# Sort steps of a graph-attention kernel: a row step in three instructions, and a third key buffer

## The chip, the cores and the metric

The kernel runs on one core of one Trainium2 chip. The metric is the device time of one execution in microseconds (us). DVE is the vector engine, ACT the scalar engine, PE the matrix engine, POOL the GpSimd engine and SP the sync engine; each works through its own queue in program order.

## What is computed

A graph-attention layer over 4096 nodes of 64 features, 50,000 random edges and 4 heads. Cut to what matters:

```python
x_proj[h] = x @ weight[h]
score[h, i] = leaky_relu(att_src[h] . x_proj[h, src[i]] + att_dst[h] . x_proj[h, dst[i]], 0.2)
output[h, dst[i]] += exp(score[h, i]) * x_proj[h, src[i]]        # over all edges i
output[h, d] /= sum(exp(score[h, i]) for edges i with dst[i] == d) + 1e-8
```

The order in which edges are added up is free, so the kernel sorts them into groups of source and destination nodes first.

## The kernel before

The edges lie as 391 keys in each of 128 partitions (`EL` = 391, padded to `L` = 512 columns with a large constant). A bitonic network sorts them: `rows` sorts every partition by itself, `runs` merges the rows of 4 neighbouring partitions, the sorted keys go to memory (`store`), parts of them are fetched again by indirect DMAs (`fetch`, on POOL), and a second stage (`pairs`, `rows(9)`, `runs`) sorts those. After it 32 blocks of destination nodes are worked through: one-hot matrices on DVE, gathers and sums as matmuls on PE, copies on ACT.

A step of the network compares two halves of each block of 2h columns. `flip` (line 197) opens a merge level k and reads the second half backwards, `half` (line 206) does the steps below it. Each step is two DVE `tensor_tensor` instructions over the whole width, first the minimum, then the maximum, and goes from one of two buffers, `sA` and `sB`, to the other. The next step reads what both wrote. `rows(1, EL)` (line 236, called in line 786) runs the levels k = 1 to 9. Levels 1 to 3 (6 steps) are 392 columns wide, levels 4 to 7 (22 steps) 384, because 391 is less than 8 over a multiple of 128; level 8 opens with a `flip` over all 512 columns, which takes up the 8 columns left out (lines 199 to 204, width `L`). An instruction handles one half of each block, so its width in elements is 196 or 192 in levels 1 to 7 and 256 in the `flip` of level 8.

All instructions are issued in the order in which the program names them (`manual_schedule`). On POOL this order is: constants (lines 87 to 156), two small DMAs of padding (lines 160, 163), a memset of `below` (line 291), and then what `tables` (line 408, called in line 785, one line ahead of `so.rows`) puts there: a memset, eight DMAs into `attbd` (line 419), a memset, and four DMAs into `Wbd` (line 424). `rows` itself puts nothing on POOL; the next POOL instruction is the `fetch` after the first sort.

The waits between instructions, also between two on one engine, are generated from the regions of the tiles that they read and write.

Of the kernel before, what the change touches and what calls it, by code (L numbers as in the profile page):

```python
# [16 lines left out]
OP = mybir.AluOpType  # L17
# [17 lines left out]
def av(a, off, *dims):  # L35

    return dataclasses.replace(a, offset=a.offset + off, ap=[list(a.ap[0])] + [list(d) for d in dims])
# [3 lines left out]
def kernel(ctx: ExitStack, tc: tile.TileContext, x: bass.AP, edge_index: bass.AP,  # L41
                         weight: bass.AP, att_src: bass.AP, att_dst: bass.AP, out: bass.AP):
    nc = tc.nc
    V, S, G, T = nc.vector, nc.scalar, nc.gpsimd, nc.tensor
# [135 lines left out]
    class Sorter:  # L180


        def __init__(self, pool):
            self.a = [None, pool.tile([P, L], F32, name="sA"), pool.tile([P, L], F32, name="sB")]
            self.y = pool.tile([P, L], F32, name="sY")
            self.z = pool.tile([P, L], F32, name="sZ")

        def begin(self, first):
            self.a[0] = first
            self.cur = 0  # L190
# [36 lines left out]
        def opposed(self, j):  # L227
# [4 lines left out]
            for o, op in ((0, OP.min), (h, OP.max)):  # L232
                V.scalar_tensor_tensor(out=av(d[:], o, [2 * h, n], [1, h]), in0=av(s[:], h, [2 * h, n], [1, h]),
                                       scalar=-1.0, in1=av(s[:], 0, [2 * h, n], [1, h]), op0=OP.mult, op1=op)

        def rows(self, first, n=L):

            w8 = -(-n // 8) * 8
            w128 = n // 128 * 128 if n % 128 <= 8 else L
            for k in range(first, 10):  # L240
                w = w8 if k <= 3 else w128 if k <= 7 else L
                self.flip(k, w)
                for j in range(k - 2, -1, -1):
                    self.half(j, w if k <= 7 or j > 6 else w128 if j > 2 else w8)
                if k == 3:
                    kept = self.cur
                if k == 7 and first <= 3:
                    assert self.cur == kept

        def turn(self):  # L250

# [33 lines left out]
    def store(skey, t):  # L285
        nc.sync.dma_start(out=skey[0, 0:P * L].rearrange("(p e) -> p e", p=P), in_=t[:])

    def below(pool, v, n, nbnd, nt, room):

        sgn = pool.tile([P, room + 1], F32, name="sgn")  # L290
        G.memset(sgn[:, 0:1], float(n))
        junk = pool.tile([P, n], F32, name="junk")
        for b in range(1, nt + 1):
            S.activation(out=junk[:], in_=v, func=ACTF.Sign, bias=nbnd[:, b:b + 1], scale=1.0,  # L294
                         accum_out=sgn[:, b:b + 1])
        if room > nt:
            S.copy(out=sgn[:, nt + 1:room + 1], in_=av(sgn[:], nt, [0, room - nt]))
        return sgn

    def counts(pp, sgn, nt, sels):  # L300

        ps = pp.tile([P, len(sels), nt + 1], F32, name="cnt_ps")
        for i, sel in enumerate(sels):
            T.matmul(out=ps[:, i, :], lhsT=sel, rhs=sgn[:], start=(i == 0), stop=True, skip_group_check=True)  # L304
        return ps

    def bounds(pool, ps):

        cnt = pool.tile([P, SETS, NR + 1], F32, name="cnt")
        pick = [pool.tile([P, SETS, NR], F32, name=f"pick{o}") for o in range(2)]  # L310
        sum = [pool.tile([P, SETS], F32, name=f"sum{o}") for o in range(2)]
        sides = (ws1, we1)
        steps = [lambda: V.tensor_scalar(out=cnt[:], in0=ps[:], scalar1=-0.5, scalar2=RUN1 * EL / 2, op0=OP.mult,
                                         op1=OP.add)]
        for f in (lambda o: V.tensor_tensor(out=pick[o][:], in0=cnt[:, :, o:o + NR],
                                            in1=av(m16[:], 0, [0, SETS], [1, NR]), op=OP.mult),
                  lambda o: V.tensor_reduce(out=sum[o][:], in_=pick[o][:], axis=AX, op=OP.add),
                  lambda o: V.tensor_tensor(out=sides[o][:], in0=sum[o][:], in1=off1[:], op=OP.add)):
            steps += [lambda f=f, o=o: f(o) for o in range(2)]
        steps.append(lambda: V.tensor_copy(out=wi1[:], in_=ws1[:]))  # L320
        return [lambda keys, f=f: f() for f in steps]
# [436 lines left out]
    key = cst.tile([P, L], F32)  # L758
    raw = cst.tile([P, L], F32)
    so = Sorter(cst)  # L760
    first = ExitStack()
    so1 = first.enter_context(tc.tile_pool(name="sort1", bufs=1))
    pr = first.enter_context(tc.tile_pool(name="pre", bufs=1))
    with tc.tile_pool(name="pps", bufs=2, space=PSUM) as pps, tc.tile_pool(name="pp1", bufs=1, space=PSUM) as pp1:
        sli = so1.tile([P, EL], I32)
        uF = so1.tile([P, EL], F32)
        dF = so1.tile([P, EL], F32)
        kF = so1.tile([P, EL], F32)
        so.begin(key)
        for t in (key, so.a[2]):  # L770
            V.memset(t[:, EL:L], KPAD)
        sgn = below(so1, av(eS[:], 0, [2, EL]), EL, nb1, NR, NR)
        for e, n in ((0, EH), (EH, EL - EH)):
            src = av(eS[:], 2 * e, [2, n])
            dst = av(eD[:], 2 * e, [2, n])
            c = slice(e, e + n)

            V.tensor_scalar(out=sli[:, c], in0=src, scalar1=2 * N - SG, scalar2=None, op0=OP.bitwise_and)
            V.tensor_scalar(out=dF[:, c], in0=dst, scalar1=float(N // 2), scalar2=-float((N - 1) * SG), op0=OP.is_ge,
                            op1=OP.mult)  # L780
            V.scalar_tensor_tensor(out=uF[:, c], in0=sli[:, c], scalar=float(N - 1), in1=src, op0=OP.mult, op1=OP.add)
            V.scalar_tensor_tensor(out=kF[:, c], in0=dst, scalar=float(2 * SG), in1=dF[:, c], op0=OP.mult, op1=OP.add)
            V.tensor_tensor(out=key[:, c], in0=uF[:, c], in1=kF[:, c], op=OP.add)
        cps = counts(pp1, sgn, NR, [sel1[:, i, :] for i in range(SETS)])
        tables(pr, pps, pp1)
        so.rows(1, EL)
        store(skey1, so.runs(RUN1, between=bounds(so1, cps)))
# [129 lines left out]
```

## Time and profile before

| | |
|---|---|
| time, median of 3 runs | 277.17 us (276.71 to 280.39) |
| the profiled execution: time, span | 276.81 us, 275.0 us |
| busy: PE, DVE, ACT, POOL | 74%, 91%, 68%, 15% of the span |
| `tensor_tensor` of line 212 (both buffers) | 202 instructions, 70.2 us |

The busy shares are means over stages of different kind. The first 57 us are the sort, where DVE is busy nearly throughout; from about 122 us on PE and DVE are both busy nearly throughout with the blocks.

### The profile page before, as it was taken

The numbers are of one execution on the slowest core, as the hardware profiler recorded it, in microseconds if no ns is written. First come the engines' busy times: TensorE is split into PE (matmuls) and PEld (weight loads), VectorE is DVE, ScalarE is ACT, GpSimd is POOL, SyncE is SP. The second block draws the span as 40 slices with busy tenths as digits, with TensorE's granted clock in tenths as the row PEclk, the third lists the DMA queues.
The fourth block names the chain that finished last, engine by engine and source line by source line (L and its number), as shares of the span: only waits on it lengthen the run. The fifth ranks groups of instructions, "written<-read, shape, count | busy, mean of one in ns | idle before, by whom it ended". The sixth has DMA issues, their size and how long they took to land.

```text
span 275.0 us, 8348 instructions
## 1 busy us (share of the span) xinstructions
PE 204.5 (74%) x3455; PEld 191.8 (70%) x3455; DVE 250.3 (91%) x521; ACT 186.1 (68%) x381; POOL 42.1 (15%) x83
## 2 busy tenths in 40 slices
PE   0011699992000197779999999999999999999992
PEld 0011479992000044579999999999999999999991
DVE  5999999935999999779999999999999999999991
ACT  1980550007999805787887888888888888888861
POOL 7885000014000000602314033000000000000000
PEclk9999995555555589999999999999999999999998
DMA  4008000011000000187394954976687768566011
GB/s 116 0 2 170 4 0 2 0 38 39 0 0 0 0 2 31 47 325 318 107 396 154 378 203 149 375 269 238 212 299 249 279 216 303 213 263 244 23 42 44
DMA packets 12763, 39.53 MB, mean 144 GB/s; under 512 B 2160, under 2 KB 8496, under 8 KB 8880
## 3 DMA queue, kind: packets, MB, share of 16 engines
q1 hardware_dynamic: 10176, 36.78, 36.4%
q10 hardware_dynamic: 1840, 1.58, 2.4%
q0 software_dynamic: 704, 0.59, 1.0%
q8 instruction: 28, 0.46, 0.7%
q14 instruction: 15, 0.12, 0.1%
HBM read 33.96 MB, written 4.98 MB: 142 GB/s over the span
## 4 chain that ended last, share of the span: by engine, by line
PE 54%; DVE 34%; DMA 5%; ACT 2%; issue 2%; POOL 0%; DVEq 0%; SPq 0%; POOLq 0%
PE acc L630 20%; DVE sA L212 13%; DVE sB L212 12%; PE ps L543 10%; PE pf L710 6%; PE ps L541 6%; PE ps L547 6%; PE acc L620 4%; DMA bc<-gat_bins 2%; DMA eS<-in_edge_index_dram 1%; DVE sA L201 1%; DVE sB L253 1%; ACT bc L508 1%; DMA raw<-gat_sorted,wi 1%; DVE sA L203 1%
## 5 line engine op out<-in xcount | busy, mean ns | idle before, releaser
L551 ACT CAST xs<-ps 128x1200 bf16<-128x1200 f32 (+1 forms) x96 | 100.8, 1050 | 0.0
L567 DVE TENSOR_TENSOR val<-xs,wv 128x4096 bf16<-128x4096 bf16 x30 | 68.4, 2281 | 0.1
L630 PE MATMUL acc<-xs,val 128*128 128x128 bf16 x992 | 60.7, 219 | 0.1
L543 PE MATMUL ps<-adb,oh 128*128 128x136 bf16 x512 | 59.5, 223 | 0.0
L541 PE MATMUL ps<-xa,oh 128*128 128x72 bf16 x512 | 56.9, 196 | 2.2 <-ACT bc L508 1.1
L630 PEld LDWEIGHTS <-val 128*128 128x128 bf16 x992 | 56.0, 98 | 0.6 <-DVE val L567 0.5
L543 PEld LDWEIGHTS <-oh 128*128 128x128 bf16 x512 | 47.5, 98 | 1.5 <-issue 1.4
L541 PEld LDWEIGHTS <-oh 128*128 128x128 bf16 x512 | 45.5, 98 | 1.4 <-DVE oh L520 1.4
L520 DVE TENSOR_SCALAR oh<-bc,pF 128x4096 bf16<-128x4096 bf16 (+2 forms) x36 | 41.1, 1141 | 2.8 <-ACT bc L508 1.8
L304 PE MATMUL cnt_ps<-sgn,sel 128*128 128x17 f32 (+1 forms) x10 | 2.5, 379 | 51.5 <-issue 31.9
L304 PEld LDWEIGHTS cnt_ps<-sgn,sel 128*128 128x128 f32 x10 | 2.3, 325 | 51.5 <-issue 51.5
L549 ACT ACTIVATE ex<-ps 128x96 bf16<-128x96 f32 (+1 forms) x96 | 24.3, 253 | 20.0 <-PE ps L547 19.9
L212 DVE TENSOR_TENSOR sA<-sB 128x256 f32<-128x256 f32 (+3 forms) x102 | 35.4, 388 | 1.5
L212 DVE TENSOR_TENSOR sB<-sA 128x256 f32<-128x256 f32 (+3 forms) x100 | 34.8, 389 | 1.5
L547 PE MATMUL ps<-xa,oh 128*128 128x72 bf16 x512 | 32.3, 197 | 0.0
L547 PEld LDWEIGHTS <-oh 128*128 128x128 bf16 x512 | 25.5, 99 | 0.1
L446 PEld LDWEIGHTS at_ps<-uv,xT 64*128 64x128 f32 x128 | 25.2, 304 | 0.2 <-issue 0.2
L446 PE MATMUL at_ps<-uv,xT 64*128 64x4 f32 x128 | 25.3, 334 | 0.0
L522 DVE TENSOR_SCALAR oh<-bc,pF 128x2048 bf16<-128x2048 bf16 (+2 forms) x36 | 24.9, 691 | 0.0
L294 ACT ACTIVATE junk<-kr,nb 128x512 f32<-128x512 f32 x32 | 23.1, 722 | 1.1
L710 PE MATMUL pf<-Wbd,aT 128*128 128x128 f32 x124 | 21.2, 293 | 0.0
L620 PEld LDWEIGHTS <-xs 128*128 128x128 bf16 x496 | 17.4, 96 | 0.4
(148 smaller groups left out, 248.9 us busy)
## 6 DMA issues: line engine op xcount, KB each, us to landing
bc<-gat_bins SPq DMA_DIRECT2D x30, 1024.0 KB, 5.9
out_dram<-res SPq DMA_DIRECT2D x31, 128.0 KB, 3.5
eD<-in_edge_index_dram ACTq DMA_DIRECT2D x2, 195.0 KB, 4.0
eS<-in_edge_index_dram SPq DMA_DIRECT2D x2, 195.0 KB, 3.8
gat_sorted<-sA SPq DMA_DIRECT2D x1, 256.0 KB, 2.0
gat_sorted<-ki SPq DMA_DIRECT2D x1, 256.0 KB, 2.0
gat_bins<-tb SPq DMA_DIRECT2D x4, 64.0 KB, 1.9
attbd<-in_att_src_dram POOLq DMA_DIRECT2D x4, 0.2 KB, 4.7
```

The lines of the kernel that those rows point to most:

```text
L212: V.tensor_tensor(out=av(d[:], at + o, [2 * h, n], [1, h]), in0=av(s[:], at, [2 * h, n], [1, h]), in1=av(s[:], at + h, [2 * h, n], [1, h]) ...
L446: T.matmul(out=ps[:, b, :], lhsT=nodes(b), rhs=uv[:, k, :], start=(b == 0), stop=True, skip_group_check=True)
L520: V.tensor_scalar(out=oh[:, e], in0=bc[:, e], scalar1=pF[:, 0:1], scalar2=None, op0=OP.is_equal)
L522: V.tensor_scalar(out=av(oh[:], (2 * NT + t0) * W2, [W2, nt], [1, W2]), in0=av(bc[:], (2 * t0 + 1) * W2, [2 * W2, nt], [1, W2]), scalar1=p ...
L541: T.matmul(out=ps[:, i, P:P + XC], lhsT=hot(2 * t + 1), rhs=xa[:, 2 * t, :], start=(i % 2 == 0), stop=False, skip_group_check=True)
L543: T.matmul(out=ps[:, i, 0:S0], lhsT=hot(2 * t), rhs=adb[:, b, :], start=False, stop=False, skip_group_check=True)
L547: T.matmul(out=ps[:, i, P:P + XC], lhsT=hot(2 * NT + t), rhs=xa[:, 2 * t + 1, :], start=False, stop=True, skip_group_check=True)
L551: S.copy(out=xs[:, t0:t0 + n, 0:P + XC], in_=ps[:, 0:n, 0:P + XC])
L567: V.tensor_tensor(out=av(val[:], 0, [Dout, H], [C, NT], [1, Din]), in0=av(xs[:], S0, [0, H], [XW, NT], [1, Din]), in1=av(wv[:], 0, [2, H * ...
L620: T.matmul(out=self.acc[:, 2 * BD:AW], lhsT=xs[:, t, 0:P], rhs=av(wv[:], 2 * (t - t0), [2 * n, H]), start=(t == 0), stop=(t == NT - 1), sk ...
L630: T.matmul(out=self.to[k], lhsT=val[:, t, k * P:(k + 1) * P], rhs=xs[:, t, 0:BD], start=False, stop=(t == NT - 1), skip_group_check=True)
L710: T.matmul(out=self.pf[0:t.shape[-1], k * P:(k + 1) * P], lhsT=t, rhs=Wbd[:, k, :], start=(k == 0), stop=True, skip_group_check=True)
```

## The change

In `rows`, levels 1 to 7 no longer use `flip` and `half` but a new `apart`. It issues three instructions instead of two: the minimum over the left 192 columns (128 in level 7), the maximum over all columns, and the minimum over the columns that are left. The buffers become three (`sA`, `sB`, and `sZ`, which `runs` uses as scratch later), taken in turn. Levels 8 and 9 keep `flip` and `half` over `sA` and `sB`. After level 3 the keys lie in the third buffer and the 8 columns that levels 4 to 7 leave out are copied from it to `sA` by a POOL instruction (`G.tensor_copy`), since level 7 ends in `sA` and level 8 reads it there. The padding of the second buffer moves to `sA`.

```diff
+            self.a.append(self.z)
...
+        def apart(self, k, j, width):
+
+
+            s, self.cur = self.a[self.cur], self.cur % 3 + 1
+            d = self.a[self.cur]
+            h = 1 << j
+            n = width // (2 * h)
+            m = (128 if k == 7 else 192) // (2 * h)
+            mirror = j == k - 1
+            for b, c, op in ((0, m, OP.min), (0, n, OP.max), (m, n - m, OP.min)):
+                at = 2 * h * b
+                o = h if op == OP.max else 0
+                if mirror:
+                    in0 = av(s[:], at + o, [2 * h, c], [1, h])
+                    in1 = av(s[:], at + 2 * h - 1 - o, [2 * h, c], [-1, h])
+                else:
+                    in0 = av(s[:], at, [2 * h, c], [1, h])
+                    in1 = av(s[:], at + h, [2 * h, c], [1, h])
+                V.tensor_tensor(out=av(d[:], at + o, [2 * h, c], [1, h]), in0=in0, in1=in1, op=op)
...
             for k in range(first, 10):
                 w = w8 if k <= 3 else w128 if k <= 7 else L
-                self.flip(k, w)
-                for j in range(k - 2, -1, -1):
-                    self.half(j, w if k <= 7 or j > 6 else w128 if j > 2 else w8)
+                if k <= 7:
+                    for j in range(k - 1, -1, -1):
+                        self.apart(k, j, w)
+                else:
+                    self.flip(k, w)
+                    for j in range(k - 2, -1, -1):
+                        self.half(j, w if j > 6 else w128 if j > 2 else w8)
                 if k == 3:
-                    kept = self.cur
-                if k == 7 and first <= 3:
-                    assert self.cur == kept
+                    assert first <= 3 and self.cur == 3
+                    if w128 < w8:
+                        G.tensor_copy(out=self.a[1][:, w128:w8], in_=self.a[3][:, w128:w8])
+                if k == 7:
+                    assert self.cur == 1
...
-        for t in (key, so.a[2]):
+        for t in (key, so.a[1]):
             V.memset(t[:, EL:L], KPAD)
```

## Rows read from the trace of the kernel before

**Rows 1.** The chain that ended last, in order of time: start us, us, what.

```profile
0.84 3.47 DMA eS<-in_edge_index_dram
...
56.80 0.73 DVE sA L212 x2
57.54 2.02 DMA gat_sorted<-sA
```

**Rows 2.** Timeline of DVE, levels 1 to 8: start us, us, engine, line, operation.

```profile
7.20 0.36 DVE L201 TENSOR_TENSOR sA<-key 128x196 f32<-128x196 f32 x1
...
7.88 0.36 DVE L201 TENSOR_TENSOR sB<-sA 128x196 f32<-128x196 f32 x1
...
17.41 0.36 DVE L201 TENSOR_TENSOR sB<-sA 128x192 f32<-128x192 f32 x1
17.68 0.35 DVE L203 TENSOR_TENSOR sB<-sA 128x192 f32<-128x192 f32 x1
18.07 0.63 DVE L212 TENSOR_TENSOR sA<-sB 128x192 f32<-128x192 f32 x2
...
26.01 0.42 DVE L201 TENSOR_TENSOR sA<-sB 128x256 f32<-128x256 f32 x1
```

**Rows 3.** Timeline of DVE in the merge of rows, where small instructions stand between steps.

```profile
50.36 0.76 DVE L212 TENSOR_TENSOR sA<-sB 128x256 f32<-128x256 f32 x2
51.03 0.22 DVE L313 TENSOR_SCALAR cnt<-cnt_ps 128x68 f32<-128x68 f32 x1
51.17 0.75 DVE L212 TENSOR_TENSOR sB<-sA 128x256 f32<-128x256 f32 x2
51.84 0.21 DVE L315 TENSOR_TENSOR pick<-cnt,m 128x64 f32<-128x64 f32 x1
51.98 0.75 DVE L212 TENSOR_TENSOR sA<-sB 128x256 f32<-128x256 f32 x2
```

**Rows 4.** Timeline of DVE where an instruction reads what the last but one wrote.

```profile
4.54 0.27 DVE L779 TENSOR_SCALAR dF<-eD 128x195 f32<-128x195 int32 x1
4.73 0.35 DVE L781 SCALAR_TENSOR_TENSOR uF<-sli,eS 128x195 f32<-128x195 int32 x1
5.00 0.38 DVE L782 SCALAR_TENSOR_TENSOR kF<-eD,dF 128x195 f32<-128x195 int32 x1
...
114.06 0.26 DVE L467 TENSOR_SCALAR t<-win 128x128 int32<-128x128 int32 x1
114.24 0.21 DVE L468 TENSOR_SCALAR t<-win 128x128 int32<-128x128 int32 x1
114.38 0.21 DVE L471 CAST tb<-t 128x128 bf16<-128x128 int32 x1
```

**Rows 5.** Timeline of POOL, the end of its queue ahead of the fetch.

```profile
16.39 0.46 POOL L162 CAST padi<-pad 1x128 int32<-1x128 f32 x1
...
21.75 0.52 POOL L419 DMA_DIRECT2D attbd<-in_att_dst_dram  x1
22.25 0.34 POOL L421 MEMSET Wbd<- 128x256 f32 x1
22.89 1.54 POOL L424 DMA_DIRECT2D Wbd<-in_weight_dram  x3 [0.29 <-POOL Wbd L421]
27.36 0.52 POOL L424 DMA_DIRECT2D Wbd<-in_weight_dram  x1 [2.94 <-DMA attbd<-in_att_dst_dram]
```

**Rows 6.** POOL's groups by form to 60 us: count, busy us, mean ns, idle before.

```profile
L98 POOL CAST b_f<-b_i 128x1 f32<-128x1 int32 x3 | 0.6, 187 | 0.0
```

**Rows 7.** Timeline of ACT and DVE: a result handed from ACT to DVE.

```profile
110.79 1.15 ACT L551 CAST xs<-ps 128x1200 bf16<-128x1200 f32 x1
...
111.98 0.96 DVE L582 TENSOR_TENSOR val<-xs,wv 128x1536 bf16<-128x1536 bf16 x1 [0.53 <-ACT xs L551]
```

**Rows 8.** Timeline of DVE and POOL, side by side in levels 2 to 5.

```profile
8.55 0.36 DVE L212 TENSOR_TENSOR sA<-sB 128x196 f32<-128x196 f32 x1
8.63 0.33 POOL L143 TENSOR_SCALAR boff<-p_f 128x1 f32<-128x1 f32 x1
8.83 0.35 DVE L212 TENSOR_TENSOR sA<-sB 128x196 f32<-128x196 f32 x1
...
13.29 0.41 DVE L212 TENSOR_TENSOR sB<-sA 128x192 f32<-128x192 f32 x1
13.70 0.73 POOL L153 TENSOR_SCALAR sel<-ioF,p_f 128x128 f32<-128x128 f32 x1
14.00 0.41 DVE L201 TENSOR_TENSOR sA<-sB 128x192 f32<-128x192 f32 x1
```

## The prediction

> **What bounds the kernel now.** I read the chain that ended last first, because a change to the sort can only count where the chain runs through it. The chain leaves the load of the edges at 4.31 us (0.84 + 3.47) and stays on DVE until the keys are stored at 57.54 us [rows 1]. So in this stretch a microsecond more or less on DVE moves all that follows: the store, the fetch, the second sort and the blocks each start when the one before them has delivered, and I found no slack in the chain behind 57.54 us that could take up a shift.
>
> Then I read DVE's timeline through the part that is changed. The 28 steps of levels 1 to 7 run from 7.20 us to the opening of level 8 at 26.01 us, 18.81 us or 0.67 us a step [rows 2]. Inside one step the reader should look at starts, not at durations. The minimum starts at 17.41 us and lasts 0.36 us, yet the maximum starts at 17.68 us, 0.09 us before the minimum has ended. The next step starts at 18.07 us, 0.04 us after the maximum has ended [rows 2]. So two instructions that don't need each other follow at 0.27 us, and one that needs the instruction just ahead follows at 0.39 us. The step of 0.66 us is 0.27 + 0.39, and the price of the dependence is 0.12 us a step.
>
> Last I read POOL's queue, because the change puts one instruction there. POOL is 15% busy, which looks harmless, but it works in order, and in this stretch it ends late: its last DMA into `Wbd` waits 2.94 us for the landing of an earlier one, is issued at 27.36 us and takes 0.52 us, so POOL is free at 27.88 us [rows 5]. That is later than 26.01 us.
>
> **The change, part by part: the three instructions.** What does one more independent instruction cost? Two small ones stand between the steps of the later merge: the one of 68 elements starts at 51.03 us and the next step at 51.17 us, so it takes 0.14 us of DVE's time though it lasts 0.22 us; the one of 64 elements takes 0.14 us too (51.84 to 51.98) [rows 3]. Between 68 elements at 0.14 us and 192 at 0.27 us [rows 2, 3] the slope is 0.13 us / 124 = 1.05 ns an element, and 0.07 us remain as a fixed part. The new step has 96 + 192 + 96 elements: 384 x 1.05 ns + 3 x 0.07 us = 0.61 us, an estimate, if none of the three ever waits. Against 0.66 us that saves 0.04 to 0.05 us a step.
>
> Do they wait? The left minimum of a step reads only columns below 192 (or 128), which the left minimum and the maximum of the step before wrote; the right minimum that stands just ahead of it wrote the others. The maximum needs the right minimum, two instructions back. With three buffers no one overwrites what a neighbour still reads. Two things must hold. A dependence two back must be free: `kF` reads what `dF`, two ahead of it, wrote, and starts 0.27 us after its neighbour of 195 elements, which is the price without a dependence; the merge step behind the 68-element instruction also reads what lies two back [rows 3, 4]. And the wait must go by columns, not by the whole tile: the cast of line 471 reads one part of `t` just behind the instruction that writes the other part, and starts 0.14 us after it, 0.07 us before that one ends [rows 4]. Both hold.
>
> [...]
>
> From both sides, the 28 steps: at best 28 x 0.05 = 1.4 us less. Against it, POOL's larger instructions take a turn between DVE's. Beside each of the five 128x128 ones (lines 153 and 156) a DVE minimum lasts 0.41 instead of 0.36 us and the step 0.71 us (13.29 to 14.00) [rows 8]; so far that turn falls into the 0.12 us in which DVE stands between two steps, which the new steps no longer have. Five times 0.12 us is 0.6 us lost. The first step gains up to 0.12 us, since its left half needs only keys of the first load, and level 8 pays 0.12 us, since it needs the last instruction. So DVE would stand ready for level 8 between 24.6 and 25.4 us, 0.6 to 1.4 us earlier than before.
>
> **The copy on POOL.** Level 8's first instruction is the `flip` over 512 columns. Its second operand reads columns 511 down to 384, and so the 8 columns that POOL's copy brings to `sA`. The copy is issued after level 3 in program order, but on POOL it stands behind everything that `tables` has put there, the twelve DMAs among it. Its source is ready at about 11 us; that doesn't help, since the queue is in order. POOL is free at 27.88 us. An instruction behind a DMA starts at once: the memset of line 421 starts at 22.25 us where the DMA before it ends at 22.27 us [rows 5]. The operation itself isn't in the trace. Its nearest rows are a POOL cast of one column at 0.19 us on average [rows 6] and one of 128 elements beside a busy DVE at 0.46 us [rows 5]. I take 0.22 us, because 8 columns are near to one and DVE stands still then. Handing a result from one engine to DVE takes 0.04 us (110.79 + 1.15 = 111.94, start 111.98) [rows 7]. So level 8 starts at 27.88 + 0.22 + 0.04 = 28.14 us; with the upper price, 28.38 us.
>
> That is 28.14 - 26.01 = **2.1 us later than before**, whatever the steps gain: DVE is ready at 25.4 us at the latest and waits 2.7 to 3.5 us. Behind the waiting instruction on DVE stands the whole rest of the sort, for which the store and the fetch wait. POOL's own times shouldn't move: the wait that makes it late ends with a DMA's landing, and the loads around it are issued by ACT and POOL, neither of which waits for DVE there. The buffers of levels 8 and 9 and of `runs` only swap names, same widths and counts: nothing. The memset moves from one tile to another of the same size ahead of the edges' arrival: nothing.
>
> Sum: 276.81 (time of the profiled execution) + 2.1 = 278.9 us. Its median stands at 277.17, 0.36 above; I predict between the two bases, **279.1 us**.
>
> **The rivals.**
> *A: the copy is in place in time.* Were POOL's wait of 2.94 us gone, the copy would be done at 25.2 us, and level 8 would start when DVE is ready: 0.6 to 1.4 us gained, 275.5 to 276.6 us. For it: a landing can come earlier in other executions. Against: the order of the queue, and that it takes nearly the whole 2.9 us. 10%.
> *B: each of the three waits for the one ahead, the other side.* If the waits went by whole tiles, or the overlap vanished, each instruction would cost its duration of 0.25, 0.36 and 0.25 us (0.22 us for 68 elements [rows 3], 28 more at 1.05 ns), and with a wait 0.03 us more each: 0.86 to 0.95 us a step, level 8 at 31.3 to 33.8 us, 5.3 to 7.8 us later: 282.1 to 285 us, up to 3% slower. It decides from 0.75 us a step on ((28.1 - 7.2) / 28); below that POOL's lateness covers it, so one extra wait a step (0.73 us) wouldn't show in the time at all. Against it: [rows 3, 4]. 5%.
> *C: POOL gets no turn while DVE runs without a pause.* The instruction of line 143 reads SBUF beside a running minimum; it ends at 8.96 us, 0.13 us after DVE has gone on from the minimum to the maximum at 8.83 us without any pause [rows 8]. So a change of instructions is enough for a turn, and the new steps have more of them. If a pause were needed after all, POOL's queue from about 7.3 us on would only go on when DVE stops at about 25 us, and its remaining 20.6 us (to 27.88), or 17.7 without its wait, would end at 43 to 46 us: 17 to 20 us slower, 294 to 297 us. 3%.
> [...]
>
> **How the numbers follow.** The forecast has 80%: within it 278.3 to 280.2 us, from the copy's price (0.19 to 0.46 us), a landing that shifts by half a microsecond, and the two bases (276.8, 277.2). A 10%, B 5%, C 3%, and 2% for what I haven't seen. Reaching down to A gives 275.6 to 280.2 us, which leaves out B, C and some edges. About 2% is what a measurement of this kernel can tell from no change. The forecast (0.8%) and A (0.4%) are within it; slower by over 2% are C, most of B and half the unseen, 8%; faster has no mechanism: 1%.
>
> **What would show it.** In the changed kernel's profile: the `flip` of level 8 preceded by 2.7 to 3.5 us of idle DVE, released by a POOL copy into `sA` that starts near 27.9 us; steps of 0.61 to 0.63 us with starts 0.17, 0.27 and 0.17 us apart, and no idle time between them; the store near 59.7 us instead of 57.5. Wrong would be: no such wait (A), steps of 0.75 us or more (B), the POOL instructions of lines 143 to 156 standing until 25 us (C), or a shift at 57.5 us that is gone by the end.

## The result and the profile after

The changed kernel takes 281.44 us (median of 6 runs, 280.69 to 281.82) beside 277.46 us for the kernel before (6 runs): ratio 1.0137, 95% interval 1.0098 to 1.0176, 4 us slower. The prediction was 279.1 us with a range up to 280.2. Its direction and its place were right, its size was half of what was measured. The ratios, here and below, are taken over executions outside a slower state (one of 337.37 us, at a granted clock of 0.66, is left out in the run with the copy on DVE), and they aren't the quotients of the medians.

| | before | after |
|---|---|---|
| time, median | 277.46 us | 281.44 us |
| span of the profiled execution | 275.0 us | 279.6 us |
| 28 steps of levels 1 to 7, first start to last end | 7.20 to 25.97 us | 6.95 to 24.62 us |
| start of level 8 | 26.01 us | 30.50 us |
| POOL's cast of the padding (line 162) | 0.46 us | 3.59 us |
| first keys of the second sort read | 64.45 us | 68.86 us |

The timeline of DVE in the changed kernel, in the columns of [rows 2]: four instructions of level 6, the last step of level 7 (three instructions merged into one row) and the opening of level 8.

```profile
17.18 0.24 DVE L255 TENSOR_TENSOR sB<-sA 128x96 f32<-128x96 f32 x1
17.35 0.34 DVE L255 TENSOR_TENSOR sB<-sA 128x192 f32<-128x192 f32 x1
17.62 0.24 DVE L255 TENSOR_TENSOR sB<-sA 128x96 f32<-128x96 f32 x1
17.79 0.24 DVE L255 TENSOR_TENSOR sZ<-sB 128x96 f32<-128x96 f32 x1
...
23.94 0.68 DVE L255 TENSOR_TENSOR sA<-sZ 128x64 f32<-128x64 f32 x3
30.50 0.42 DVE L202 TENSOR_TENSOR sB<-sA 128x256 f32<-128x256 f32 x1 [5.88 <-POOL sA L273]
```

The steps do what the change says: starts 0.17, 0.27 and 0.17 us apart, each before the last one has ended, 0.61 us a step against 0.66 us in [rows 2]. Then DVE stands for 5.88 us and waits for POOL's copy. The timeline of POOL shows why it is so late; beside it belongs [rows 5].

```profile
16.98 3.59 POOL L162 CAST padi<-pad 1x128 int32<-1x128 f32 x1
20.88 0.52 POOL L163 DMA_DIRECT2D gat_sorted<-padi  x1 [0.31 <-POOL padi L162]
...
27.08 0.52 POOL L446 DMA_DIRECT2D attbd<-in_att_dst_dram  x1 [1.58 <-DMA gat_sorted<-padi]
27.59 0.33 POOL L448 MEMSET Wbd<- 128x256 f32 x1
28.21 2.05 POOL L451 DMA_DIRECT2D Wbd<-in_weight_dram  x4 [0.29 <-POOL Wbd L448]
30.26 0.21 POOL L273 COPY sA<-sZ 128x8 f32<-128x8 f32 x1
```

The cast that took 0.46 us in [rows 5] takes 3.59 us. It ends 3.7 us later than before (20.57 instead of 16.85), and the DMAs behind it on POOL are issued later. The 2.94 us that the last of them waited in [rows 5] are gone, another waits 1.58 us instead: 3.7 - 2.94 + 1.58 = 2.3 us, and POOL is free at 30.26 us instead of 27.88.

That sum hides when the waits end. In ten profiles of this case (both kernels and all runs but the two with memsets ahead of the cast) POOL waits in this stretch for the landing of a DMA of its own, and that wait ends between 26.59 and 27.36 us, whether the cast is quick, late or gone. What differs is what POOL has still to issue then: with the cast quick or gone one or two DMAs, in the changed kernel one DMA into `attbd`, the memset and four DMAs into `Wbd`, 3.2 us (27.08 to 30.26). The DMA of the padding landed 1.6 us after its issue in the kernel before; issued 3.7 us later it takes 5.9 us. That the large load of `x`, issued by ACT at 18.6 us and landing 7.9 us later, holds these landings would fit, but no run moved it, so it is only argued.

The chain that ended last, in the columns of [rows 1], which before led from the load of the edges through DVE alone to the store, now runs through POOL:

```profile
12.03 3.01 POOL sel L153 x4
16.98 3.60 POOL padi L162
20.88 5.92 DMA gat_sorted<-padi
28.21 2.05 POOL Wbd L451 x4
62.03 2.02 DMA gat_sorted<-sB
```

Behind level 8 nothing gives the delay back: 4.49 us at level 8, 4.41 at the first keys of the second sort, 4.6 in the span.

### The profile page after: what moved, and what is told of

It is laid out like the page before. It is cut to its first block, busy times and chain, and to the rows that moved or that the text cites. A ratio compares the mean times of both kernels' runs of the same rounds, so it can differ in the third digit from the quotient of the medians.

```text
span 279.6 us, 8377 instructions
## 1 busy us (share of the span) xinstructions
PE 205.5 (73%) x3455; PEld 192.5 (69%) x3455; DVE 250.1 (89%) x549; ACT 186.2 (67%) x381; POOL 46.1 (16%) x84
## 3 DMA queue, kind: packets, MB, share of 16 engines
q10 hardware_dynamic: 1840, 1.58, 2.5%
## 4 chain that ended last, share of the span: by engine, by line
PE 53%; DVE 26%; POOL 8%; DMA 6%; issue 3%; ACT 2%; SPq 0%; POOLq 0%; DVEq 0%
PE acc L657 19%; PE ps L570 10%; DVE sA L213 10%; DVE sB L213 10%; PE pf L737 6%; PE ps L568 6%; PE ps L574 6%; PE acc L647 4%; DMA gat_sorted<-padi 2%; DMA bc<-gat_bins 2%; POOL padi L162 1%; POOL sel L153 1%; DVE sB L280 1%; ACT bc L535 1%; DMA raw<-gat_sorted,wi 1%
## 5 line engine op out<-in xcount | busy, mean ns | idle before, releaser
L213 DVE TENSOR_TENSOR sA<-sB 128x256 f32<-128x256 f32 (+3 forms) x80 | 28.4, 396 | 1.2
L213 DVE TENSOR_TENSOR sB<-sA 128x256 f32<-128x256 f32 (+3 forms) x80 | 28.4, 396 | 1.1
L473 PEld LDWEIGHTS at_ps<-uv,xT 64*128 64x128 f32 x128 | 25.9, 312 | 0.2 <-issue 0.2
L473 PE MATMUL at_ps<-uv,xT 64*128 64x4 f32 x128 | 25.9, 339 | 0.0
```

The source lines that it names most:

```text
L213: V.tensor_tensor(out=av(d[:], at + o, [2 * h, n], [1, h]), in0=av(s[:], at, [2 * h, n], [1, h]), in1=av(s[:], at + h, [2 * h, n], [1, h]) ...
L473: T.matmul(out=ps[:, b, :], lhsT=nodes(b), rhs=uv[:, k, :], start=(b == 0), stop=True, skip_group_check=True)
```

## The experiments

From the two traces I took this theory into the runs: the wait for POOL's copy is all that makes the kernel slower; about half of it comes from POOL's queue as it was (predicted), the other half from the cast, which finds no turn beside a DVE that no longer pauses between steps (by a turn I mean no more than that a POOL instruction that reads is done within about one of DVE's steps). The rival: POOL's end depends on the landings of DMAs, which differ from execution to execution, and the cast has no part in it.

**The wait alone.** The kernel before, with two-instruction steps and their pauses, and one POOL copy added:

```diff
                 if k == 3:
                     kept = self.cur
+                    if first <= 3 and w128 < w8:
+                        t = self.a[kept]
+                        G.tensor_copy(out=t[:, w128:w8], in_=t[:, w128:w8])
```

> The kernel before with one thing added: after level 3 a POOL copy of the 8 columns onto themselves, which level 8 then has to wait for; the steps keep two instructions and their pauses. Theory: POOL's cast takes 0.46 us as before, POOL is free at 27.9 us, level 8 opens at 28.1 us instead of 26.0, ratio 1.008: this is the share of the wait by itself. Rival (the wait costs the full 4 us whatever the steps do): level 8 near 30 us, ratio 1.014.

Measured: 279.51 us, ratio 1.0085 (1.006 to 1.0111). Timelines of POOL and DVE of this kernel:

```profile
16.54 0.47 POOL L162 CAST padi<-pad 1x128 int32<-1x128 f32 x1
...
28.34 0.21 POOL L249 COPY sB<-sB 128x8 f32<-128x8 f32 x1
```

```profile
28.58 0.42 DVE L201 TENSOR_TENSOR sA<-sB 128x256 f32<-128x256 f32 x1 [3.12 <-POOL sB L249]
```

The cast is quick again and level 8 opens at 28.58 us. So the wait that the prediction counted is there and costs about what it said, with the old steps too: 2.6 us at level 8 in this execution, in which POOL's DMAs ended 0.5 us later than in [rows 5], and 0.85% of the time.

**The copy on DVE.** The changed kernel without the wait for POOL:

```diff
                         self.apart(k, j, w)
+                        if (k, j) == (4, 3) and w128 < w8:
+                            V.tensor_copy(out=self.a[1][:, w128:w8], in_=self.a[3][:, w128:w8])
...
-                    if w128 < w8:
-                        G.tensor_copy(out=self.a[1][:, w128:w8], in_=self.a[3][:, w128:w8])
```

> The changed kernel with the copy of the 8 columns on DVE, behind the first step of level 4, instead of on POOL. Theory (the wait for POOL is all that makes the change slower, and the three-instruction steps do gain): no idle time ahead of level 8, which opens at 24.7 to 24.8 us, 1.2 to 1.3 us earlier than in the kernel before; time 275.5 to 276.2 us, ratio 0.995, although POOL's cast still takes its 3.6 us. Rival (what DVE gains is lost behind it, because POOL's late tables or something else bind next): ratio 1.000 or above.

Measured: median 276.41 us beside 276.8 for the kernel before, ratio 0.9947 (0.9917 to 0.9976). Timeline of DVE:

```profile
11.16 0.16 DVE L267 COPY sA<-sZ 128x8 f32<-128x8 f32 x1
11.24 0.68 DVE L255 TENSOR_TENSOR sB<-sA 128x96 f32<-128x96 f32 x3
...
23.94 0.68 DVE L255 TENSOR_TENSOR sA<-sZ 128x64 f32<-128x64 f32 x3
24.66 0.43 DVE L202 TENSOR_TENSOR sB<-sA 128x256 f32<-128x256 f32 x1
```

Level 8 opens at 24.66 us, 1.35 us earlier than in [rows 2], although the cast lasts 4.03 us here. At level 8 the three-instruction steps gain what they promise, and without the wait for POOL the kernel is a little faster than before instead of slower; how much of the 1.35 us reaches the time, the interval (0.2 to 0.8%) and the medians (0.4 us) leave open. The copy itself occupies DVE for 0.08 us (11.16 to 11.24).

**The cast without its read.** If the cast is the other half, a memset in its place should bring back the predicted 2.1 us.

```diff
-    G.tensor_copy(out=padi[:], in_=pad[:, 0:W2])
+    G.memset(padi[:], int(KPAD))
```

> The changed kernel with one POOL instruction replaced: the cast of the padding (line 162, 128 elements on one partition, 3.59 us in the changed kernel) becomes a memset, which reads nothing. Theory (the copy is late because POOL's queue is, and 2.4 us of its lateness come from this cast, which finds no turn beside a DVE that runs without pauses): the next DMA is issued near 17.3 us, the end of POOL's queue is as in the kernel before, level 8 opens near 28.1 us instead of 30.50, and the time is 2.1 us above the kernel before, ratio 1.008. Rival (the 2.4 us come from the landings of the DMAs, which differ from execution to execution): level 8 near 30.5 us, ratio 1.014.

Measured: 278.74 us, ratio 1.0043 (1.0013 to 1.0073). Timelines of POOL and DVE:

```profile
16.91 0.19 POOL L162 MEMSET padi<- 1x128 int32 x1
...
27.84 0.20 POOL L273 COPY sA<-sZ 128x8 f32<-128x8 f32 x1
```

```profile
28.07 0.43 DVE L202 TENSOR_TENSOR sB<-sA 128x256 f32<-128x256 f32 x1 [3.60 <-POOL sA L273]
```

Level 8 opens at 28.07 us; the prediction had 28.14. The medians lie 1.9 us apart (278.74 and 276.8), close to the expected 2.1; the ratio lies below the expected 1.008. The ten executions spread from 276.69 to 279.69 us, and the profiled one is the slowest of them. That the landings vary from one to the next would fit, but no profile of a shorter one was taken, so it is only argued.

**Two pauses.** The same changed kernel, cast and all, but the first two steps of level 6 in two instructions:

```diff
+            parts = ((0, m, OP.min), (0, n, OP.max), (m, n - m, OP.min))
+            if k == 6 and j >= 4:
+                parts = ((0, n, OP.min), (0, n, OP.max))
-            for b, c, op in ((0, m, OP.min), (0, n, OP.max), (m, n - m, OP.min)):
+            for b, c, op in parts:
```

> The changed kernel with the first two steps of level 6 in two instructions, minimum and maximum over all columns, so that each of these steps ends with a pause of DVE, at about 17.2 and 17.9 us, as in the kernel before. Theory (POOL's cast waits for a pause of DVE): the cast starts near 17.0 us and ends within one pause, by 17.4 to 18.0 us, level 8 opens near 28.1 us, ratio 1.008. Rival (the cast waits for something else, such as the other widths of level 7): the cast still ends near 20.6 us, level 8 near 30.5 us, ratio 1.014.

Measured: 279.21 us, ratio 1.0072 (1.0043 to 1.0102). Timelines of POOL and DVE:

```profile
16.95 0.48 POOL L162 CAST padi<-pad 1x128 int32<-1x128 f32 x1
```

```profile
16.65 0.63 DVE L258 TENSOR_TENSOR sA<-sZ 128x192 f32<-128x192 f32 x2
17.31 0.62 DVE L258 TENSOR_TENSOR sB<-sA 128x192 f32<-128x192 f32 x2
...
28.28 0.43 DVE L202 TENSOR_TENSOR sB<-sA 128x256 f32<-128x256 f32 x1 [3.55 <-POOL sA L276]
```

With the two steps back in their old form the cast takes 0.48 instead of 3.59 us, at the price of 0.1 us on DVE that level 8 never sees. It ends at 17.43 us, 0.1 us behind the pause at 17.28 to 17.31 us, as it does in the kernel before (below). These steps have other widths too (192 and 192 elements), and no run parts the pause from the widths. The extra 2.2 us are settled all the same: the new stream of steps delays the cast, the cast delays the issues behind it, and they delay the copy.

**Which instructions are passed over.** That doesn't yet say why the cast falls through, when the POOL instructions ahead of it got turns beside DVE instructions without any pause (the four of line 153 took 3.03 us, 0.76 us each, the one of line 156 took 0.72 us). Of those that read, it is the only one on a single partition. So the cast over all partitions:

```diff
-    pad = cst.tile([1, W1], F32)
+    pad = cst.tile([P, W1], F32)
...
-    padi = cst.tile([1, W2], I32)
+    padi = cst.tile([P, W2], I32)
...
```

> The changed kernel with POOL's cast of the padding over all 128 partitions instead of one, the same 128 elements in each. Theory (POOL gets no turn for this cast beside a DVE without pauses, however many partitions it has): it lasts 3 us or more, level 8 near 30.5 us. Rival (only an instruction on one partition is passed over; all POOL instructions that got their turn in this stretch had 128 partitions): it lasts 0.5 to 0.8 us, level 8 near 28.2 us.

Measured: one execution, 278.65 us beside 277.0. Timelines of POOL and DVE:

```profile
16.42 0.34 POOL L162 CAST padi<-pad 128x128 int32<-128x128 f32 x1
```

```profile
16.54 0.34 DVE L255 TENSOR_TENSOR sZ<-sB 128x96 f32<-128x96 f32 x1
...
27.74 0.43 DVE L202 TENSOR_TENSOR sB<-sA 128x256 f32<-128x256 f32 x1 [2.98 <-POOL sA L273]
```

It ends at 16.76 us, and the DVE instruction that starts beside it lasts 0.34 instead of 0.25 us. That looked like the answer, but this cast also starts at another moment: 0.12 us ahead of DVE's next instruction, where the cast in the changed kernel starts 0.03 us ahead of one. Three small memsets on POOL ahead of the cast change the moment, once with one partition and once with 128:

```diff
+    spare = cst.tile([P, 1], F32)
...
+    for i in range(3):
+        G.memset(spare[:], 0.0)
     G.tensor_copy(out=padi[:], in_=pad[:, 0:W2])
```

> The changed kernel with three memsets of one column put ahead of POOL's cast on one partition, which start it about 0.1 us later against DVE's steps (so far it starts 0.03 us ahead of DVE's next instruction). Theory (what matters is that the cast runs on one partition): still passed over, 3 us or more, level 8 near 30.5 us. Rival (what matters is the moment in DVE's step at which it asks): a turn within one step, 0.3 to 0.8 us, level 8 near 28.2 us.

> The kernel with the cast over 128 partitions, shifted by three memsets in the same way, so that it starts about as close ahead of DVE's next instruction as the cast in the changed kernel (before, 0.12 us ahead). Theory (the partitions matter): a turn within one step, 0.3 to 0.8 us, level 8 near 28 us. Rival (the moment matters): passed over until level 7, 3 us or more, level 8 near 30 us.

Measured: 281.38 and 281.76 us beside 278.83, one execution each. Timelines of POOL, one partition, then 128:

```profile
17.33 3.22 POOL L165 CAST padi<-pad 1x128 int32<-1x128 f32 x1
```

```profile
17.23 3.22 POOL L165 CAST padi<-pad 128x128 int32<-128x128 f32 x1
```

Both are passed over for 3.22 us. The one over 128 partitions started together with a DVE maximum (both at 17.23 us), not 0.03 us ahead of an instruction as I had aimed for. The two casts over 128 partitions are the same instruction on the same data, one at 0.34 and one at 3.22 us: the theory of the single partition has fallen. What differs between them is the moment of the start, and that three memsets instead of a DMA stand just ahead of the cast. The cast of the changed kernel was passed over behind a DMA too, so the memsets aren't needed for it; that the moment decides is likely, but not shown apart from them.

Last the widths. In all six profiles where the cast is passed over, it ends between 20.45 and 20.68 us. In the changed kernel that is at 20.57 us, in the first step of level 7, whose left minimum has 64 instead of 96 elements and which takes 0.70 instead of 0.61 us:

```profile
20.21 0.78 DVE L255 TENSOR_TENSOR sA<-sZ 128x64 f32<-128x64 f32 x3
20.91 0.68 DVE L255 TENSOR_TENSOR sB<-sA 128x64 f32<-128x64 f32 x3
```

With these widths at every level:

```diff
-            m = (128 if k == 7 else 192) // (2 * h)
+            m = 128 // (2 * h)
```

> The changed kernel with the left minimum over 128 columns at every level (64, 192 and 128 elements an instruction), as it has it in level 7, where the cast got its turn at last, between the left minimum and the maximum. Theory (the turn needs a moment in which DVE's next instruction isn't ready yet, and behind a left minimum of 64 elements the maximum is released late enough for that): the cast ends within one step, by 17.8 us, level 8 near 28.2 us. Rival (only the change of level, with its other order of instructions, opened the turn): the cast lasts until the next level, level 8 later than 29.5 us.

Measured: one execution, 279.85 us beside 277.0. Timelines of POOL and DVE:

```profile
16.94 0.42 POOL L162 CAST padi<-pad 1x128 int32<-1x128 f32 x1
```

```profile
28.60 0.42 DVE L202 TENSOR_TENSOR sB<-sA 128x256 f32<-128x256 f32 x1 [4.01 <-POOL sA L273]
```

The cast takes 0.42 us, as expected (level 8 opens 0.4 us later than expected, since POOL's wait for a landing ended only at 27.34 us), but the mechanism that I had expected isn't shown: the cast started at a moment of its own again (16.94 us), and which of DVE's instructions it ended beside is open. So what stays open is the rule by which a POOL read finds its turn in a stream of overlapping DVE instructions. The runs show that at widths of 96, 192 and 96 it can fail for 3.2 to 4.2 us (in six of seven profiles), and that it didn't fail in the three profiles in which the steps around the cast are of the old form, with a pause at the end of each.

**A version that beats both.** In the run with the copy on DVE, the keys of the second sort were there 1.33 us earlier, but ACT started its part only 0.32 us earlier (67.03 against 67.35 us), since a copy of 3.6 us stood ahead of it. Timeline of ACT in the kernel with the copy on DVE:

```profile
63.54 3.61 ACT L477 COPY adb<-identb 128x4096 bf16<-128x4096 bf16 x1
67.03 0.73 ACT L421 ACTIVATE kr<-raw,goff 128x512 f32<-128x512 f32 x1
```

That copy needs nothing that comes late, so it was moved ahead of ACT's wait for PE:

```diff
+        S.copy(out=adb[:, :, 0:P], in_=av(identb[:], 0, [0, ND], [1, P]))
         for k, (n, nodes, to) in enumerate(...):
...
-        S.copy(out=adb[:, :, 0:P], in_=av(identb[:], 0, [0, ND], [1, P]))
```

> The kernel with the copy on DVE, and on ACT the copy of the identity into adb (3.6 us) moved ahead of its wait for PE's tables. Theory (of the 1.3 us gained at level 8 part was lost because ACT started the counts of the second sort at 67.0 us, held by that copy, and PE's warm-up ended at 106.5 us behind them, 2 us after DVE was ready): the counts start when the fetched keys land, near 63.2 us, the warm-up ends near 102 us, and the time is 1.3 us or a little more below the kernel before, ratio 0.993 to 0.995. Rival (the second sort on DVE alone sets the time there): the same as with the DVE copy alone.

Measured: 275.78 us (275.29 to 276.48) beside 277.0, ratio 0.9953 (0.993 to 0.9977). Timeline of ACT:

```profile
65.72 0.72 ACT L421 ACTIVATE kr<-raw,goff 128x512 f32<-128x512 f32 x1 [2.51 <-issue]
```

ACT's part starts 1.3 us earlier than with the DVE copy alone, and not at 63.2 us, as I had expected: it reads all four parts of the keys, and with the DVE copy alone the DMA of the last was issued only at 62.97 us. The ratios of the two versions lie within each other's intervals, so the order on ACT isn't shown to matter for the time. Finally the three-instruction step in 31 more steps:

```diff
-        def apart(self, k, j, width):
+        def apart(self, k, j, width, left=0):
...
-            m = (128 if k == 7 else 192) // (2 * h)
+            m = (left or (128 if k == 7 else 192)) // (2 * h)
...
                     self.flip(k, w)
                     for j in range(k - 2, -1, -1):
-                        self.half(j, w if j > 6 else w128 if j > 2 else w8)
+                        if first == 9 and j > 0:
+                            self.apart(k, j, L, L // 2)
+                        else:
+                            self.half(j, w if j > 6 else w128 if j > 2 else w8)
...
-            for j in range(8, -1, -1):
-                self.half(j)
+            self.half(8)
+            for j in range(7, -1, -1):
+                self.apart(9, j, L, L // 2)
...
-                    self.half(j, to=to if end and j == last else None)
+                    if end or j == 8:
+                        self.half(j, to=to if end and j == last else None)
+                    else:
+                        self.apart(9, j, L, L // 2)
...
```

> The kernel of the run before in this call (copy on DVE, other order on ACT), with three instructions also in 31 further steps of 512 columns: the merges of rows that have no small instructions between their steps, and level 9 of the second sort. Theory: 0.75 instead of 0.795 us a step, 1.2 to 1.4 us less, ratio 0.989 to 0.991. Rival (DVE isn't what the second sort waits for): nothing, ratio 0.994.

Measured: 275.54 us (273.95 to 279.57), ratio 0.9951 (0.9915 to 0.9988). Timeline of DVE in a merge of rows:

```profile
43.42 0.83 DVE L255 TENSOR_TENSOR sA<-sZ 128x128 f32<-128x128 f32 x3
44.15 0.83 DVE L255 TENSOR_TENSOR sB<-sA 128x128 f32<-128x128 f32 x3
```

A step takes 0.73 us where the two-instruction steps of the run before take 0.80 (starts at 41.23, 42.02 and 42.82 us), and the spans of the two profiled executions are 272.4 and 274.0 us (the first is the second shortest of its ten). The times of all executions don't show it: leaving out the longest, they spread from 273.95 to 277.92 us, and the two ratios are the same within their intervals.

## Why the prediction was wrong in size

**What bounds the kernel: right.** The delay at level 8 passes through to the end (4.49 us there, 4.6 in the span).

**The three instructions: right.** Predicted 0.61 us a step and DVE ready at 24.6 to 25.4 us; measured 0.61 us and 24.62. POOL's five large instructions cost 0.09 us each (a step of 0.70 us), so that DVE was ready at the early end. With each instruction at its whole duration a step would have been 0.86 us, the lower end of rival B; no run shows that, and in the steps of 0.61 us each instruction starts before the last one has ended.

**The copy behind POOL's queue: right as a mechanism.** The copy lasts 0.21 us (predicted 0.22) and DVE goes on 0.03 us later (predicted 0.04). By itself this wait costs 0.85% with the old steps, and 1.7 to 2.6 us at level 8 with the new ones in the four runs in which the cast was quick or gone.

**"POOL's own times shouldn't move": here it failed.** This term put POOL's end at 27.88 us; it was 30.26, because the cast took 3.59 instead of 0.46 us. I had looked for waits on DVE among the semaphores and found none. But the cast stood for 3.59 us without one: with a memset of 0.19 us, which reads nothing, in its place, POOL's copy was done at 28.04 us. The rows for that were on the table: in rival C I took the line 143 in [rows 8], which got its turn at a change of instructions, to mean that any POOL read gets one at any change. One instruction of one column doesn't show that. The cast in [rows 5], 0.46 us long and ended 0.1 us behind DVE's pause between two steps at 16.71 to 16.75 us, was the row to ask: what would it do without that pause? Timeline of DVE in the kernel before, beside it:

```profile
16.08 0.63 DVE L212 TENSOR_TENSOR sB<-sA 128x192 f32<-128x192 f32 x2
16.75 0.63 DVE L212 TENSOR_TENSOR sA<-sB 128x192 f32<-128x192 f32 x2
```

**The rivals.** C was the right neighbour with the wrong extent: not all of POOL's reads starve until DVE stops, one does, until 20.57 us in level 7, and with the DMAs behind it that is 2.3 us instead of 17 to 20. It should have stood as a case of degree, a few microseconds, with a chance to match, and the range should have reached up to it. A would have been the outcome with the copy on another engine: 24.66 us at level 8, within its bounds. As the prediction words it, with POOL's copy done at 25.2 us, it couldn't have gained more than 0.8 of its 0.6 to 1.4 us, since level 8 needs the copy. B didn't happen.

The cast didn't stand behind a single DVE instruction: in the changed kernel 17 of them started between the start of the cast at 16.98 us and the maximum at 20.35 us, which lasted 0.44 instead of 0.34 us and in which the cast ended at 20.57 us.

## What to carry to other kernels

When instructions of one engine are packed without gaps, ask who lived in the gaps: here a cast on another engine, off the path, slipped by more than three microseconds with no semaphore between the two, and whatever stood behind it in its queue slipped too. A small operation put on an idle engine was as late here as what stood ahead of it in that engine's queue (it started at 30.26 us; its source was written by 10.71 us); look up where the queue stands at that moment, not the engine's busy share. For 8 columns, 0.08 us on the busy engine was cheaper than a wait of 5.9 us for the idle one.

## What the runs showed of the hardware that I had not expected

A POOL cast of 128 elements that takes 0.34 to 0.48 us where it gets a turn took 3.2 to 4.2 us beside back-to-back DVE instructions of 96, 192 and 96 elements in six of seven profiles, on one partition and on 128. DVE instructions that depend on the last but one follow each other at about 1.05 ns an element and 0.07 us, 0.17 us for 96 elements and 0.27 us for 192, without any wait between them for 17.7 us.
